# Two-half encoder trunk in split fp32: more pulled steps inside the normalisation chains, and a running LayerNorm sum in PSUM

## The chip, the cores and the metric

The kernel runs on one core of one Trainium2 chip. The metric is device time in microseconds. The kernel before took 1223.17 us (median of three runs, 1222.43 to 1230.81). Matmuls run on TensorE (PE), elementwise work on VectorE (DVE) and ScalarE (ACT), the splitting of weights on GpSimd (POOL), and nearly all transfers are issued by SyncE (SP).

## The reference

The input x is 512 positions by 1024 channels in fp32. Two layers are computed, and every sub-layer is x = x + RMSNorm(f(RMSNorm(x))).

```python
for i in range(DEPTH):                       # DEPTH = 2
    h = rms_norm(x, g[0])
    if i % 2 == 0:
        m = parallel_conv_mla(h, ...)        # short convolution beside latent attention
    else:
        m = conformer_conv(h, ...)           # pw1 -> GLU -> conv 31 -> LayerNorm -> silu -> pw2
    x = x + rms_norm(m, g[1])
    h = rms_norm(x, g[2])
    x = x + rms_norm(squared_relu_mlp(h, mlp_w1[i], mlp_w2[i]), g[3])

def conformer_conv(h, w_pw1, b_pw1, w_dw, b_dw, ln_g, ln_b, w_pw2, b_pw2):
    u = h @ w_pw1 + b_pw1
    a, g = jnp.split(u, 2, axis=-1)
    u = a * jax.nn.sigmoid(g)
    u = depthwise_conv(u, w_dw) + b_dw       # 31 taps per channel
    u = jax.nn.silu(layer_norm(u, ln_g, ln_b))   # LayerNorm over the 1024 channels
    return u @ w_pw2 + b_pw2
```

## The kernel before, in words

**Layout and arithmetic.** Channels lie on the 128 partitions in 8 tiles, positions along the free axis. Each fp32 operand is split into a high and a low part (`fp32r`), and each product is three matmuls (lines 244 to 246: high x high, low x high, high x low), so one output tile of 128 channels over 1024 input channels is a group of 24 matmuls. `strip` (line 208) fetches a weight strip of 128 x 1024, copies its high part on ACT (line 221) and subtracts it on POOL (line 222).

**The halves.** The positions are cut into half A (0 to 255) and half B (256 to 511). From the convolution on, A is 240 wide (`A2`) and B 272 wide (`B2`), since the 31 taps reach over the cut. All work of the second part of the program is a list of steps in the table `M2` (line 35): `up` and `down` are one output tile of an MLP product for one half (24 matmuls each), `pw1` is one tile of the gated product (48 matmuls), `pw2` one tile of the product after the LayerNorm. Between them stand the **chains** `join`, `norm` and `finish`: a sum of squares over all channels, a root, and a pass over eight tiles ("chunks") which gives the next product its input.

**A chain** is serial: the sum over partitions is a few matmuls with a column of ones (`done`, line 340; here called the SUM), the root is some twelve tiny instructions on DVE (`rstd`, lines 361 to 392), the result is spread over the partitions by matmuls with the identity (`spread`, line 406; the SPREAD), and then come the chunks: `join` has lines 444 to 462 before an MLP and 444 to 486 before another product, `layer_norm` lines 831 and 841 to 845. To keep PE busy meanwhile, the chain **pulls** steps of the other half out of the list and writes them into its own instruction stream. How many is set by `pace` (line 289): each chunk adds its estimated time to a clock, and one step is pulled whenever 2.9 us have come together (`STEP_US`, line 38).

**What sets the order.** In `M2` DVE works in the order in which the program writes its instructions. PE, ACT and POOL also work in order, in an order that the scheduler settles when the program is built. An `up` step is the group on PE, a relu on ACT (line 498), the square, a copy of the high part on ACT (line 228) and the subtraction on DVE (line 234), which is the last to read the step's PSUM bank. `up_step` (line 867) has the square done by ACT (line 500) while a convolution is under way, and otherwise by DVE (line 502). Groups inside a chain use only the three PSUM banks called S, since the banks pj, o and mi serve as the chain's scratch.

**Convolution.** The 31 taps per channel tile are 31 DVE instructions (lines 804 and 809) on a PSUM accumulator. They are dealt out between the steps by `fill` (line 274): each step gives a credit (`FILL`, line 40), and each tap costs `TAP_US` = 0.475 of it. When a `norm` chain begins, `layer_norm` adds up the eight convolved tiles on POOL (lines 820 and 821, executed at line 317) for the mean.

Of the kernel before, what the change touches and what calls it, by code (L numbers as in the profile page):

```python
# [34 lines left out]
M2 = [('up', 'A', 0, 0, 0, 8), ('join', 'B', 0, 1), ('down', 'A', 0, 0, 0, 8), ('up', 'A', 0, 1, 0, 8), ('down', 'A', 0, 1, 0, 8), ('up', 'A', 0, 2, 0, 8), ('down', 'A', 0, 2, 0, 8), ('up', 'A', 0, 3, 0, 8), ('down', 'A', 0, 3, 0, 8), ('join', 'A', 0, 3), ('up', 'B', 0, 0, 0, 8), ('down', 'B', 0, 0, 0, 2), ('pw1', 'A', 0, 4), ('down', 'B', 0, 0, 2, 6), ('pw1', 'A', 4, 8), ('down', 'B', 0, 0, 6, 8), ('up', 'B', 0, 1, 0, 8), ('down', 'B', 0, 1, 0, 8), ('up', 'B', 0, 2, 0, 8), ('norm', 'A'), ('down', 'B', 0, 2, 0, 8), ('pw2', 'A', 0, 8), ('join', 'A', 1, 1), ('up', 'B', 0, 3, 0, 8), ('down', 'B', 0, 3, 0, 8), ('join', 'B', 0, 3), ('up', 'A', 1, 0, 0, 8), ('down', 'A', 1, 0, 0, 8), ('pw1', 'B', 0, 3), ('up', 'A', 1, 1, 0, 8), ('pw1', 'B', 3, 6), ('down', 'A', 1, 1, 0, 8), ('pw1', 'B', 6, 8), ('up', 'A', 1, 2, 0, 8), ('down', 'A', 1, 2, 0, 8), ('norm', 'B'), ('up', 'A', 1, 3, 0, 8), ('pw2', 'B', 0, 8), ('join', 'B', 1, 1), ('down', 'A', 1, 3, 0, 8), ('up', 'B', 1, 0, 0, 8), ('down', 'B', 1, 0, 0, 6), ('finish', 'A'), ('down', 'B', 1, 0, 6, 8), ('up', 'B', 1, 1, 0, 8), ('down', 'B', 1, 1, 0, 8), ('up', 'B', 1, 2, 0, 8), ('down', 'B', 1, 2, 0, 8)]
# [94 lines left out]
def trunk(ctx: ExitStack, tc: tile.TileContext, a, out: bass.AP):  # L130
# [170 lines left out]
    class Sum:
# [128 lines left out]
    def join(xs, ms, s, post, pre, hs, seg, h, mlp):  # L430
# [695 lines left out]
```

## Time and profile before

| what | value |
|---|---|
| median of three runs | 1223.17 us |
| the profiled execution | 1222.25 us, of which its span is 1220.5 us |
| PE busy | 1160.9 us (95%) |
| DVE, ACT, POOL busy | 662.8, 654.1, 852.9 us (54%, 54%, 70%) |
| mean granted PE clock | 0.977 of full speed |

The page names each group by line, engine and operation; the table by stretches (the windows) gives for a piece of the span the busy time and, behind an x, the number of instructions of each engine, and then the granted PE clock. A matmul that waits is not counted as busy, and one at half clock counts as busy for twice as long, so in this kernel the number of matmuls in a stretch says more than the busy time.

### The profile page before, as it was taken

The numbers are of one execution on the slowest core, as the hardware profiler recorded it, in microseconds if no ns is written. First come the engines' busy times: TensorE is split into PE (matmuls) and PEld (weight loads), VectorE is DVE, ScalarE is ACT, GpSimd is POOL, SyncE is SP. The second block draws the span as 40 slices with busy tenths as digits, with TensorE's granted clock in tenths as the row PEclk, the third lists the DMA queues.
The fourth block names the chain that finished last, engine by engine and source line by source line (L and its number), as shares of the span: only waits on it lengthen the run. The fifth ranks groups of instructions, "written<-read, shape, count | busy, mean of one in ns | idle before, by whom it ended". The sixth has DMA issues, their size and how long they took to land.

```text
span 1220.5 us, 22995 instructions
## 1 busy us (share of the span) xinstructions
PE 1160.9 (95%) x8926; PEld 1118.3 (92%) x8926; DVE 662.8 (54%) x1707; ACT 654.1 (54%) x1181; POOL 852.9 (70%) x419
## 2 busy tenths in 40 slices
PE   7899989999999998999997989999999799999996
PEld 6788878999999998999997989999999799999995
DVE  5662699464512226678774455488896454232223
ACT  5421677466645446446456656564455666454351
POOL 5654563149888986789884848788988477778680
PEclk9899999999999999999998989999999899999998
DMA  6411332046555654455552635555556254564341
GB/s 213 148 59 38 98 100 69 2 158 211 189 189 174 205 183 149 155 191 187 187 177 90 197 99 190 171 192 192 192 185 191 72 188 156 184 179 155 117 160 37
DMA packets 55405, 184.01 MB, mean 151 GB/s; under 512 B 6400, under 2 KB 10880, under 8 KB 55296
## 3 DMA queue, kind: packets, MB, share of 16 engines
q1 hardware_dynamic: 54864, 182.00, 46.0%
q8 instruction: 70, 1.15, 0.4%
q10 hardware_dynamic: 432, 0.54, 0.1%
q14 instruction: 39, 0.32, 0.1%
HBM read 180.42 MB, written 2.10 MB: 150 GB/s over the span
## 4 chain that ended last, share of the span: by engine, by line
PE 84%; DVE 8%; ACT 4%; DMA 2%; issue 2%; POOL 1%; SPq 0%; DVEq 0%; ACTq 0%
PE S L244 21%; PE S L245 20%; PE S L246 20%; PE pj L244 6%; PE pj L245 6%; PE pj L246 6%; DMA raw<-in_win 1%; PE mi L340 1%; ACT whi L221 1%; POOL wlo L222 1%; DVE pr L744 1%; PE mi L406 1%; PE mi L747 1%; DVE s L738 1%; PE o L245 1%
## 5 line engine op out<-in xcount | busy, mean ns | idle before, releaser
L222 POOL TENSOR_TENSOR wlo<-raw,whi 128x1024 fp32r<-128x1024 f32 (+2 forms) x347 | 803.3, 2332 | 295.3 <-ACT whi L221 281.0
L221 ACT ACTIVATE whi<-raw 128x1024 fp32r<-128x1024 f32 (+2 forms) x347 | 355.9, 1030 | 405.6 <-PE S L245 198.1
L244 PE MATMUL S<-h,whi 128*128 128x256 f32 (+3 forms) x1224 | 357.6, 295 | 18.5 <-DVE hid L234 8.4
L246 PE MATMUL S<-h,wlo 128*128 128x256 f32 (+3 forms) x1224 | 357.6, 293 | 0.0
L245 PE MATMUL S<-h,whi 128*128 128x256 f32 (+3 forms) x1224 | 357.6, 293 | 0.0
L244 PEld LDWEIGHTS S<-h,whi 128*128 128x128 f32 x1224 | 235.1, 194 | 26.3 <-DVE hid L234 10.5
L246 PEld LDWEIGHTS S<-h,wlo 128*128 128x128 f32 x1224 | 236.2, 193 | 3.8 <-POOL wlo L222 0.2
L245 PEld LDWEIGHTS S<-h,whi 128*128 128x128 f32 x1224 | 236.1, 193 | 3.6 <-issue 0.2
L244 PE MATMUL S<-hid,whi 128*128 128x256 f32 (+2 forms) x808 | 227.5, 283 | 5.1 <-DVE acc L317 2.7
L245 PE MATMUL S<-hid,whi 128*128 128x256 f32 (+2 forms) x808 | 227.4, 282 | 0.0
L246 PE MATMUL S<-hid,wlo 128*128 128x256 f32 (+2 forms) x808 | 226.8, 281 | 0.0
L809 DVE SCALAR_TENSOR_TENSOR pj<-u,taps,pj 128x240 f32<-128x240 f32 (+1 forms) x464 | 192.7, 481 | 1.1
L244 PEld LDWEIGHTS S<-hid,whi 128*128 128x128 f32 x808 | 152.6, 190 | 6.7 <-DVE acc L317 3.5
L245 PEld LDWEIGHTS S<-hid,whi 128*128 128x128 f32 x808 | 153.3, 190 | 0.4 <-DVE hid L234 0.2
L246 PEld LDWEIGHTS S<-hid,wlo 128*128 128x128 f32 x808 | 153.1, 190 | 0.0
L244 PE MATMUL pj<-h,whi 128*128 128x272 f32 (+3 forms) x328 | 101.7, 310 | 6.5 <-ACT h L228 5.3
L245 PE MATMUL pj<-h,whi 128*128 128x272 f32 (+3 forms) x328 | 101.3, 309 | 0.0
L246 PE MATMUL pj<-h,wlo 128*128 128x272 f32 (+3 forms) x328 | 100.9, 308 | 0.0
L234 DVE TENSOR_TENSOR hid<-S,hid 128x256 fp32r<-128x256 f32 (+2 forms) x102 | 43.0, 421 | 62.2 <-ACT hid L228 62.2
L244 PEld LDWEIGHTS pj<-h,whi 128*128 128x128 f32 x328 | 62.5, 191 | 10.0 <-ACT h L228 5.6
L512 DVE TENSOR_TENSOR m<-S,m 128x256 f32<-128x256 f32 (+2 forms) x73 | 30.4, 417 | 70.1 <-PE S L246 70.1
L245 PEld LDWEIGHTS pj<-h,whi 128*128 128x128 f32 x328 | 62.4, 190 | 3.6 <-DVE h L231 0.9
(251 smaller groups left out, 1746.6 us busy)
## 6 DMA issues: line engine op xcount, KB each, us to landing
raw<-in_w SPq DMA_DIRECT2D x256, 512.0 KB, 3.4
raw<-in_pw SPq DMA_DIRECT2D x48, 512.0 KB, 3.5
raw<-in_win SPq DMA_DIRECT2D x16, 512.0 KB, 3.3
x<-in_xT SPq DMA_DIRECT2D x16, 256.0 KB, 4.1
raw<-in_wout SPq DMA_DIRECT2D x8, 512.0 KB, 3.3
raw<-in_wq SPq DMA_DIRECT2D x8, 192.0 KB, 2.4
out<-x SPq DMA_DIRECT2D x8, 120.0 KB, 4.1
out<-x SPq DMA_DIRECT2D x6, 136.0 KB, 1.8
```

The lines of the kernel that those rows point to most:

```text
L221: nc.scalar.activation(h, r, AF.Copy)
L222: nc.gpsimd.tensor_tensor(out=lo[:, c0:c1], in0=r, in1=h.bitcast(F32), op=ALU.subtract)
L234: eng.tensor_tensor(out=lo, in0=src, in1=hi.bitcast(F32), op=ALU.subtract)
L244: nc.tensor.matmul(acc, sh, mh, start=i == 0, stop=False)
L245: nc.tensor.matmul(acc, sh, ml, start=False, stop=False)
L246: nc.tensor.matmul(acc, sl, mh, start=False, stop=i == n - 1)
L340: nc.tensor.matmul(s[:, b : b + 1], q[:, sl.start - self.seg.lo : sl.stop - self.seg.lo], one, start=i == 0, stop=i == len(self.parts) - 1,)
L406: nc.tensor.matmul(o[:, sl], r[:, b : b + 1].to_broadcast([bw, P]), ident[:bw, :bw], start=True, stop=True,)
L512: nc.vector.tensor_tensor(out=m[seg.sl], in0=acc, in1=m[seg.sl], op=ALU.add)
L738: nc.vector.reduce_max(out=mx, in_=S, axis=AX.X)
L744: eng.tensor_scalar(out=pr_, in0=pr_, scalar1=sm, scalar2=None, op0=ALU.mult)
L809: nc.vector.scalar_tensor_tensor(out=dst, in0=src, scalar=wk, in1=acc, op0=ALU.mult, op1=ALU.add)
```

## The change

It does six things, all between the attention and the end.

1. **Holds.** A new `hold` runs at each sum and each root: it settles what is pending and pulls one step of the other half, whatever the clock says. `rstds` calls it ahead of the SUM and once more between root and SPREAD; `layer_norm` does the same around the mean, and `join` ahead of its last sum.
2. **Pace in operations.** The chain's clock counts DVE operations of 0.39 us and pulls at 2.35 us; the estimates for edges, roots and chunks are gone.
3. **Pulled squares.** `up_step` gives the square to ACT for pulled steps as well.
4. **LayerNorm's sum.** It runs along with the convolution: `Sum.run` copies the first convolved tile into the PSUM bank o on ACT and adds the others to it on DVE, each as the last action of its convolution; the last sum goes to SBUF. The POOL additions are gone, and the SUM of the mean has one part in place of two.
5. **Taps.** A tap costs 0.41 of credit in the 240-wide half and 0.44 in the 272-wide one.
6. **The table.** `M2` is reordered at the four places that the second block shows.

```diff
-STEP_US, EDGE_US, ROOT_US, CHUNK_US, SQUARE_US = 2.9, 1.0, 2.8, 1.45, 0.5
-TAP_US = 0.475
+OP_US, STEP_US = 0.39, 2.35
+TAP_US = {T // 2 - PAD: 0.41, T // 2 + PAD: 0.44}
...
+    def step():
+        if not steps or steps[0][0] or steps[0][1][1] in ("F", scope["half"]):
+            return False
+        scope["pulling"] = True
+        steps.pop(0)[2]()
+        scope["pulling"] = False
+        return True
+
+    def pace(n):
+        scope["time"] += n * OP_US
+        while scope["time"] >= STEP_US and step():
             scope["time"] -= STEP_US
         scope["time"] = min(scope["time"], STEP_US)
+
+    def hold():
+        settle()
+        if scope.get("chain") and step():
+            scope["time"] = 0.0
...
+        def run(self, t):
+            self.i += 1
+            if self.i == 1:
+                self.bank = ps("o")[:, : self.seg.w]
+                nc.scalar.activation(self.bank, t, AF.Copy)
+                self.parts = [self.bank]
+                return
+            dst = tmp("acc1")[:, : self.seg.w] if self.i == self.n else self.bank
+            self.eng.tensor_tensor(out=dst, in0=self.parts[0], in1=t, op=ALU.add)
+            self.parts = [dst]
...
     def rstds(total, ratio=None):
-        return spread(rstd(total.done(), D, ratio), total.seg)
+        hold()
+        r = rstd(total.done(), D, ratio)
+        hold()
+        return spread(r, total.seg)
...
-            pace(CHUNK_US)
+            pace(4 if mlp else 3)
...
-        vsum = Sum(NC, seg, nc.gpsimd, whole=WHOLE[1])
-        for c in range(NC):
-            vsum.add(vs[c][:, seg.sl])
+        hold()
         mu = small()[:, : seg.nb]
         nc.vector.tensor_scalar(
-            out=mu, in0=vsum.done(), scalar1=-1.0 / D, scalar2=None, op0=ALU.mult
-        )
+            out=mu, in0=vsum[seg].done(), scalar1=-1.0 / D, scalar2=None, op0=ALU.mult
+        )
+        hold()
...
-        scope["square"] = nc.scalar if convs or todo else nc.vector
+        scope["square"] = nc.scalar if convs or todo or scope.get("pulling") else nc.vector
```

```text
before: ('down','B',0,0,0,2), ('pw1','A',0,4), ('down','B',0,0,2,6), ('pw1','A',4,8), ('down','B',0,0,6,8)
after:  ('down','B',0,0,0,4), ('pw1','A',0,4), ('down','B',0,0,4,8), ('pw1','A',4,8)
before: ('norm','A'), ('down','B',0,2,0,8), ('pw2','A',0,8), ('join','A',1,1), ('up','B',0,3,0,8)
after:  ('norm','A'), ('down','B',0,2,0,8), ('up','B',0,3,0,4), ('pw2','A',0,8), ('join','A',1,1), ('up','B',0,3,4,8)
before: ('down','A',1,0,0,8), ('pw1','B',0,3), ('up','A',1,1,0,8), ('pw1','B',3,6), ('down','A',1,1,0,8)
after:  ('down','A',1,0,0,4), ('pw1','B',0,3), ('down','A',1,0,4,8), ('pw1','B',3,6), ('up','A',1,1,0,8)
before: ('down','A',1,2,0,8), ('norm','B'), ('up','A',1,3,0,8), ('pw2','B',0,8), ('join','B',1,1), ('down','A',1,3,0,8)
after:  ('norm','B'), ('down','A',1,2,0,8), ('up','A',1,3,0,4), ('pw2','B',0,8), ('join','B',1,1), ('up','A',1,3,4,8), ('down','A',1,3,0,8)
```

In each tuple the last two numbers are the range of tiles.

**What moves, place one: ACT, in the join of half A between the convolution module and the second MLP.** Names S_ are the accumulators of pulled `up` steps, y_ their relus, hid_ the copies of their high parts, whi_ weights, x_ and h_ the chain's own chunks. Before, the copy of a step stands behind the relu of a later step:

```order
L498 ACTIVATE y_8488<-S_8463 128x256
L450 ACTIVATE x_2173<-pj_8351 128x240
L459 ACTIVATE h_2189<-mi_8347 128x240
L450 ACTIVATE x_2174<-o_8393 128x240
L459 ACTIVATE h_2191<-pj_8351 128x240
L221 ACTIVATE whi_8699<-raw_8698 128x1024
L498 ACTIVATE y_8536<-S_8511 128x256
L228 ACTIVATE hid_8263<-S_8413 128x256
...
L498 ACTIVATE y_8576<-S_8551 128x256
L228 ACTIVATE hid_8265<-S_8463 128x256
```

Now relu, square and copy of one step follow each other (the lines are 22 to 27 higher in the changed file, L520 is the relu and L229 the copy):

```order
L520 ACTIVATE y_8482<-S_8457 128x256
L522 ACTIVATE S_8457<-y_8482 128x256
L229 ACTIVATE hid_7973<-S_8457 128x256
L222 ACTIVATE whi_8677<-raw_8676 128x1024
L520 ACTIVATE y_8527<-S_8502 128x256
L522 ACTIVATE S_8502<-y_8527 128x256
L229 ACTIVATE hid_7975<-S_8502 128x256
```

Over the whole program a relu stands ahead of an earlier step's copy 36 times before and 9 times now, among 128 `up` steps each.

**Place two: PE, at the second sum of the LayerNorm of half A.** Before, the SUM (L340, from the accumulated squares acc_ and sq_), the SPREAD (L406) and the first matmuls of `pw2` (inputs h_, 240 wide) follow each other:

```order
L246 MATMUL S_7896<-hid_7243,wlo_7694 128x256
L340 MATMUL mi_7867<-kst,acc_7742 128x1
L340 MATMUL mi_7867<-kst,sq_7865 128x1
...
L406 MATMUL mi_7887<-kst,s_7873 128x128 x2
L244 MATMUL S_7968<-h_2187,whi_7745 128x240
```

Now 18 matmuls of a pulled `down` step stand between SUM (L366) and SPREAD (L435), and four `up` steps of half B (96 matmuls, 256 wide) between SPREAD and `pw2`:

```order
L366 MATMUL mi_7804<-kst,sq_7770 128x1
L245 MATMUL S_7930<-hid_7257,whi_7737 128x256
...
L247 MATMUL S_7930<-hid_7267,wlo_7738 128x256
L435 MATMUL mi_7856<-kst,s_7810 128x128 x2
L245 MATMUL S_7985<-h_2187,whi_7773 128x256
...
L247 MATMUL S_8093<-h_2201,wlo_7926 128x256
L245 MATMUL pj_8129<-h_2187,whi_7980 128x240
```

**Place three: PE, at the same point of the LayerNorm of half B.** In the order before, SUM, SPREAD and `pw2` stand together as in half A. Now 39 matmuls of pulled steps lie between SUM and SPREAD, but `pw2` (272 wide) follows the SPREAD at once:

```order
L366 MATMUL mi_11621<-kst,sq_11567 128x1
L245 MATMUL S_11707<-h_2193,whi_11490 128x240
...
L247 MATMUL S_11758<-h_2201,wlo_11535 128x240
L435 MATMUL mi_11679<-kst,s_11629 128x128 x3
L245 MATMUL S_11835<-h_2187,whi_11644 128x272
```

The four `up` steps that cover half A's chunks are here pulled ahead of the SPREAD, because the rest of the taps has already taken five of the eight `down` steps.

More of the change, by code (lines that the diff above doesn't have):

```diff
@@ L32 @@
 N_RAW = 2
+PAD = 16
 M0 = [('wout', 'A'), ('join', 'A', 0, 1), ('wout', 'B')]
 M1 = []
[L35 removed]
@@ L36 @@
 M3 = [('up', 'B', 1, 3, 0, 8), ('down', 'B', 1, 3, 0, 8), ('finish', 'B')]
-STEP_US, EDGE_US, ROOT_US, CHUNK_US, SQUARE_US = 2.9, 1.0, 2.8, 1.45, 0.5
-TAP_US = 0.475
-FILL = {'up': 2.3, 'down': 2.3, 'first': 2.6, 'sum': 1.8, 'pw1': 4.8, 'pw2': 2.3, 'wout': 1.5}
+OP_US, STEP_US = 0.39, 2.35
+TAP_US = {T // 2 - PAD: 0.41, T // 2 + PAD: 0.44}
+FILL = {'up': 2.3, 'down': 2.3, 'first': 2.6, 'sum': 1.8, 'pw1': 4.8, 'pw2': 2.3}
 START = ['x', (128,), 'x', (256, 512, 768), 'x', 'x', 'x', 'x', 'x', 'x', ()]
@@ L277, in fill @@
         credit[0] += us
-        while convs and credit[0] >= TAP_US:
-            credit[0] -= TAP_US
+        while convs:
             turn[0] += 1
-            conv = convs[turn[0] % min(len(convs), 2)]
+            conv, cost = convs[turn[0] % min(len(convs), 2)]
+            if credit[0] < cost:
+                break
+            credit[0] -= cost
             if next(conv, None) is None:
-                convs.remove(conv)
+                convs.remove((conv, cost))
         if not convs:
@@ L811, in rest @@
                     )
-                yield k
-        convs.append(rest())
+                if k < CK - 1:
+                    yield k
+            vsum[seg].run(vs[c][:, seg.sl])
+            yield CK
+        convs.append((rest(), TAP_US[seg.w]))
     def layer_norm(seg):
         hv = views(hs, seg)
-        vsum = Sum(NC, seg, nc.gpsimd, whole=WHOLE[1])
-        for c in range(NC):
-            vsum.add(vs[c][:, seg.sl])
+        hold()
         mu = small()[:, : seg.nb]
         nc.vector.tensor_scalar(
-            out=mu, in0=vsum.done(), scalar1=-1.0 / D, scalar2=None, op0=ALU.mult
+            out=mu, in0=vsum[seg].done(), scalar1=-1.0 / D, scalar2=None, op0=ALU.mult
         )
+        hold()
         total = spread(mu, seg)
-        pace(EDGE_US)
         s2 = Sum(NC, seg, whole=WHOLE[2])
@@ L845, in layer_norm @@
             split((hv[c][0][seg.sl], hv[c][1][seg.sl]), t, nc.vector, late=late)
-            pace(2 * SQUARE_US)
+            pace(2)
         settle()
+    vsum = {}
     def start(c, seg):
+        if c == 0:
+            vsum[seg_of("AB"[seg is B], 1)] = Sum(NC, seg_of("AB"[seg is B], 1), nc.vector)
         if seg is A:
@@ L887, in shared_step @@
         down(kept[m], src(), ms[m], seg, first, sums[h])
-        fill(FILL["sum"])
     def pw1_step(tok, h, c):
```

33 lines of the change are left out of this document (7 added, 26 removed).

## Prediction

> **What bounds the kernel now.** I read the page first.
>
> ```profile
> PE 1160.9 (95%) x8926; PEld 1118.3 (92%) x8926; DVE 662.8 (54%) x1707; ACT 654.1 (54%) x1181; POOL 852.9 (70%) x419
> PE   7899989999999998999997989999999799999996
> PEclk9899999999999999999998989999999899999998
> ```
>
> PE sets the time; no other engine is above 70%. The slices show where it is not full: at the start and in the last slice, which the change doesn't touch, and in slices 16, 22, 24 and 32 (of 30.5 us each), with the clock down in three of these. How much is lost there the table by stretches tells, through the number of matmuls (behind the first x).
>
> ```profile
> 340.00:400.00 60.00, 60.00 (x511) 60.00 (x511) 13.04 (x31) 28.13 (x40) 49.55 (x21) 1.00 0.54 178
> 460.00:520.00 60.00, 54.64 (x439) 53.39 (x439) 41.53 (x114) 33.38 (x64) 41.62 (x18) 0.97 0.47 151
> 640.00:680.00 40.00, 31.76 (x249) 30.95 (x248) 15.64 (x52) 24.28 (x48) 22.23 (x11) 0.87 0.37 127
> 680.00:720.00 40.00, 33.99 (x243) 33.12 (x242) 22.46 (x66) 23.06 (x51) 23.41 (x10) 0.87 0.44 146
> 740.00:780.00 40.00, 38.65 (x332) 37.52 (x332) 26.16 (x80) 25.77 (x56) 29.15 (x13) 1.00 0.49 160
> 880.00:920.00 40.00, 40.00 (x359) 40.00 (x359) 37.15 (x93) 23.57 (x39) 35.63 (x18) 1.00 0.57 189
> 920.00:980.00 60.00, 51.09 (x394) 50.36 (x393) 30.92 (x86) 37.02 (x71) 36.38 (x17) 0.89 0.42 133
> 980.00:1020.00 40.00, 37.21 (x313) 36.28 (x312) 23.62 (x72) 26.37 (x55) 28.31 (x12) 1.00 0.52 166
> 1080.00:1140.00 60.00, 60.00 (x481) 60.00 (x480) 13.62 (x32) 27.61 (x42) 45.58 (x20) 1.00 0.44 142
> ```
>
> The first, sixth and last rows are undisturbed: 0.1174 us a matmul at 256 columns (60/511), 0.1114 at 240 (40/359), 0.1247 at 272 (60/481). What the other stretches lack at these rates is the loss. **a**, the join of A ahead of `pw1` (460 to 520): 511 - 439 = 72 matmuls, 8.5 us. **b**, the LayerNorm of A (640 to 680): some 62 wide and 187 narrow ones are worth 28.1 us, 11.9 lost. **c**, the join of A behind `pw2` (680 to 720): 28.4 us of work, 11.6 lost. **d**, the join of B ahead of `pw1` (740 to 780): about half of each width, 38.0, 2.0 lost. **e**, the LayerNorm of B (920 to 980): 24.4 + 21.8, 13.8 lost. **f**, the join of B behind `pw2` (980 to 1020): 35.8 at a mean of 0.1145, 4.2 lost. Together 52.0 us, all inside chains.
>
> **What PE waits for there**, from the table of waits (PE, 262 to 1200 us):
>
> ```profile
> PE S L244 <- DVE hid L234: 10.2, 10, 2.1
> PE mi L406 <- DVE s L392: 5.0, 2, 2.6
> PE mi L340 <- DVE acc L317: 4.8, 2, 3.1
> PE S L244 <- DVE u L786: 1.9, 1, 1.9
> ```
>
> **The change part by part.**
>
> *Holds in the LayerNorms (b, e).* PE's timeline, at the second sum of A's LayerNorm, then DVE's root and last chunk, and one window of the clock:
>
> ```profile
> 649.66 0.35 PE L340 MATMUL mi<-kst,acc 128*128 128x1 f32 x2 [3.14 <-DVE acc L317]
> 653.55 1.20 PE L406 MATMUL mi<-kst,s 128*128 128x128 f32 x4 [2.41 <-DVE s L392]
> 656.59 0.99 PE L244 MATMUL S<-h,whi 128*128 128x240 f32 x3 [1.85 <-ACT h L228]
> 651.18 0.16 DVE L361 TENSOR_SCALAR s<-mi 128x2 f32<-128x2 f32 x1 [1.35 <-PE mi L340]
> 653.25 0.16 DVE L392 SCALAR_TENSOR_TENSOR s<-mi,s 128x2 f32<-128x2 f32 x1
> 661.58 0.41 DVE L231 TENSOR_TENSOR h<-o,h 128x240 fp32r<-128x240 f32 x1 [0.44 <-ACT h L228]
> 652.50:655.00 2.50, 1.20 (x4) 0.93 (x4) 1.31 (x7) 0.00 (x0) 0.00 (x0) 0.50 0.03 13
> ```
>
> PE stands still for the sum, the root (651.18 to 653.41, 2.2 us) and the first chunk, and then takes the chunks at half clock as they come. Now the mean's SPREAD is followed by 81 matmuls, 9.5 us, against 7.1 us (642.6 to 649.7) of DVE work; the root has 18 matmuls beside it, 2.1 us; and the tail, 661.99 - 654.75 = 7.2 us, has four `up` steps, 96 x 0.1174 = 11.3 us. What stays open is the root. It is sometimes longer:
>
> ```profile
> 684.86 2.37 POOL L222 TENSOR_TENSOR wlo<-raw,whi 128x1024 fp32r<-128x1024 f32 x1 [0.53 <-ACT whi L221]
> 685.86 1.40 DVE L366 TENSOR_SCALAR s<-s 128x2 int32<-128x2 int32 x1
> 651.37 0.17 DVE L366 TENSOR_SCALAR s<-s 128x2 int32<-128x2 int32 x1
> ```
>
> One tiny instruction took 1.40 us and ended when POOL's subtraction did (687.23); at 651 POOL was idle and it took 0.17. Under a covered LayerNorm POOL keeps working, so I count a root of 2.2 to 4.4 us there, a wait of 0.1 to 2.3, and take 1.2. With 1.2 us for banks that the tail's steps share with the chain's scratch, b keeps 2.4 of 11.9: **-9.5**. (The Trainium skill, "SBUF — State Buffer", section "Who interferes with whom", says that DVE and GpSimd share a port pair, and whoever comes second waits for the whole instruction of the other. The trace agrees, with 687.26 against 687.23. It speaks against the change, which puts POOL work beside every root; by its worst case b would keep 3.5.)
>
> B's LayerNorm (e) has the same cover up to the SPREAD, and the root has 39 matmuls (4.3 us). Its tail has nothing:
>
> ```profile
> 954.89 1.28 ACT L844 ACT_TABLE_LOAD   x1
> 957.64 1.05 PE L244 MATMUL S<-h,whi 128*128 128x272 f32 x3 [2.89 <-ACT h L228]
> 487.66 1.01 PE L244 MATMUL S<-h,whi 128*128 128x256 f32 x3 [2.33 <-ACT h L228]
> 485.00:490.00 5.00, 2.67 (x14) 2.46 (x14) 2.50 (x7) 3.87 (x8) 3.81 (x2) 0.74 0.13 17
> 490.00:495.00 5.00, 5.00 (x41) 5.00 (x41) 3.35 (x9) 1.54 (x4) 0.88 (x1) 0.92 0.57 197
> ```
>
> The 2.9 us ahead of the first chunk stay, table load included. After the wait of 2.33 us in a the clock was 0.74 and then 0.92 over 5 us each: 2.6 + 0.8 = 3.4 us at half speed, 1.7 lost. I charge the same here, and 1.4 for the rest: e keeps 6.0 of 13.8, **-7.8**. (The Trainium skill, "TensorE: Matmul & The Clock Gate", section "Why this matters for your kernels", asks for no idle gap beyond about 3 us. By that the tail's 2.9 us might leave the clock alone, and the sum would be 1.7 lower; the row after 2.33 us disagrees.)
>
> *Pulled squares (c, and a, d).* ACT, DVE and PE in stretch c:
>
> ```profile
> 704.31 0.42 DVE L502 SCALAR_TENSOR_TENSOR S<-S,y 128x256 f32<-128x256 f32 x1
> 707.12 0.37 ACT L498 ACTIVATE y<-S 128x256 f32<-128x256 f32 x1
> 707.38 0.38 ACT L228 ACTIVATE hid<-S 128x256 fp32r<-128x256 f32 x1
> 707.79 0.42 DVE L234 TENSOR_TENSOR hid<-S,hid 128x256 fp32r<-128x256 f32 x1 [3.06 <-ACT hid L228]
> 708.26 0.39 PE L244 MATMUL S<-h,whi 128*128 128x256 f32 x1 [2.08 <-DVE hid L234]
> ```
>
> This is a circle. DVE has squared a step by 704.7; ACT may copy it only behind the relu of the step after the next, which waits for PE; DVE waits 3.06 us for the copy, with the chain's chunks queued behind, and PE 2.08 us for the bank that DVE frees. It comes again at 701 and 714. With the square on ACT the three operations stand together; only four of c's pulled steps are `up` now, the others `down`, which need one DVE addition. I leave c 3.0 (bank turns and the root), **-8.6**. In a, relu and copy stay crossed at one step; its tail has 10 matmuls behind the SPREAD and a whole `down` group further on, which shortens the wait of 2.33. The sigmoid wait of 1.9 stays, since its cause, two weight copies ahead of a table load, is in the new order too. a keeps 4.4 of 8.5, **-4.1**. d gains nothing that I can price, **0**; f has steps for its second half that were used up before, **-1.0**.
>
> *What this costs.* 30 squares go from DVE to ACT.
>
> ```profile
> 929.51 0.38 ACT L500 ACTIVATE S<-y 128x240 f32<-128x240 f32 x1
> 516.51 7.96 DVE L809 SCALAR_TENSOR_TENSOR pj<-u,taps,pj 128x240 f32<-128x240 f32 x21
> 807.78 4.17 DVE L809 SCALAR_TENSOR_TENSOR pj<-u,taps,pj 128x272 f32<-128x272 f32 x10
> L317 POOL TENSOR_TENSOR acc<-acc,m 128x272 f32<-128x272 f32 x5 | 3.9, 771 | 0.0
> ```
>
> At 0.38 us they are 11.4 us of ACT. ACT is busy 33.4 of 60 us in a and 25.8 of 40 in d, so most fit: 0 to 11.4, and I take **+2.5**.
>
> *Taps and the sum.* Taps come every 0.379 us (7.96/21) at 240 and 0.417 (4.17/10) at 272. A credit of 2.3 now buys 5.6 or 5.2 of them, 2.1 or 2.2 us of DVE, and with the 0.4 us subtraction 2.5 or 2.6 us per step, where PE needs 24 x 0.1174 = 2.8 or 24 x 0.1114 = 2.7. It fits, narrowly in B: 0. The POOL additions (12, 0.7 us each) leave an engine that isn't the bound; in their place come 14 DVE additions and two ACT copies, some 6 us that DVE has free beside the taps (37.2 of 40 us busy at the fullest): 0 to 6, I take 0. The SUM of the mean loses a part: under 1 us.
>
> **Sum.** -9.5 - 7.8 - 8.6 - 4.1 - 1.0 = -31.0; + 2.5 gives -28.5. On the profiled execution's 1222.25 us that is 1193.75; the median of the runs shown lies 0.92 above it, so I forecast 1194.7 us.
>
> **Rivals.**
>
> *The chains get longer (1209).* Each pulled step's last instruction stands on DVE ahead of the chain's next one and waits for PE. If sums and roots then come late, a SPREAD stalls PE, as L406 did twice for 2.5 us. For it: c's circle was of this kind. Against: behind a root every SPREAD but b's has at least 39 matmuls since its SUM. The six chains have twelve pairs of SUM and SPREAD; at half of that stall each, 1.2 us, they cost 14.4: 1209.
>
> *ACT takes over (1219).* If all 11.4 us of squares lie on the path, and the crossed pairs return as waits, a, c and d gain nothing: 1223.2 - 17.3 - 1.0 + 11.4 is 1216, and with b's root at its worst and the clock down once more some 1219. The rows speak against it: ACT is at 66% at most (f).
>
> *DVE falls behind the taps (1238, the other side).* A tap's duration in the table is above its spacing: 0.46 and 0.50. If the sum in PSUM or POOL's company spreads the taps to that, a step costs 5.6 x 0.46 + 0.4 + 0.1 = 3.1 and 5.2 x 0.50 + 0.5 = 3.1 us of DVE against 2.8 and 2.7: 0.3 and 0.4 us on each of some 45 steps, 31.5 us in all. Taps left over are drained when a LayerNorm begins and use up its steps: b then keeps e's 6.0 (+3.6) and e its 13.8 (+7.8). 1194.7 + 31.5 + 11.4 is 1238. It decides from 0.43 (A) and 0.42 us (B) per tap. Against: 21 taps in a row kept 0.379.
>
> *More is covered (1183).* If e's clock doesn't drop (1.7), no root meets POOL (1.2), banks never bind (1.2 in b, 1.4 in e), a and c keep only their fixed waits (4.0) and the squares are free (2.5), it is 12.0 lower.
>
> That the change doesn't pull what it says is excluded by the order of the instructions.
>
> **How the numbers follow.** Forecast 0.60, longer chains 0.15, more covered 0.10, DVE behind 0.08, ACT 0.07. The range runs from 1180, below the covered case, to 1214, past the longer chains; it leaves out the last two rivals and little else. A measurement of this kernel can tell about 1% (12 us) from no change. Faster by more: 0.60 + 0.10 + 0.12 of the longer chains = 0.82. Within 1%: 0.03 + 0.07 = 0.10. Slower: 0.08.
>
> **What would show it.** Right: stretches b and c without any window at clock 0.50, one left in e's tail with a wait near 2.9 us; L406 waits under 2 us in all; L234's waits as PE's releaser under 3 us; DVE near 95% busy while taps run, with PE at 20 of 20. Wrong: PE waits for DVE while taps run (the taps' rival), long L406 waits (the chains'), or weights and chunk copies late on ACT. The forecast fails altogether if the matmuls per 20 us in the undisturbed stretches change.

## The result, and the profile after

The changed kernel took **1191.6 us** (median of four runs, 1187.9 to 1199.8) against 1226.5 us for the kernel before (1222.4 to 1230.8): a ratio of 0.9724, 95% interval 0.9656 to 0.9792. The profiled execution took 1193.7 us, with a span of 1191.9 us. Set against the forecast of 1194.7 us that is 3.1 us less. By the ratio the gain is 25 to 42 us, in the medians 34.9, where 28.5 were forecast. So sign and size came out; but the terms of the sum were off in both directions, and two things that it put at nothing, the price of a tap and the taps that are left when a LayerNorm begins, were worth several us.

Three lines of the page: busy time of PE, its busy tenths in 40 slices of 29.8 us, and the granted clock.

```profile
PE 1149.6 (96%) x8916; PEld 1108.9 (93%) x8916; DVE 662.1 (56%) x1691; ACT 664.4 (56%) x1213; POOL 845.6 (71%) x407
PE   7899989999999999999998999999998999999996
PEclk9999999999999999999999999999989999999998
```

Of the four dips inside the convolution module's part, two are left: slice 22, the LayerNorm of A, now at full clock, and slices 30 and 31, the LayerNorm of B, where the clock is still lowered. The table by stretches shows it with numbers. The columns are the stretch, its length, the busy time and (x) the number of instructions on PE, weight loads, DVE, ACT and POOL, then the granted clock, the DMA share and GB/s.

```profile
460.00:520.00 60.00, 58.79 (x491) 58.02 (x491) 38.25 (x110) 37.98 (x75) 46.81 (x20) 1.00 0.53 172
520.00:560.00 40.00, 40.00 (x340) 40.00 (x340) 37.03 (x98) 20.59 (x32) 33.95 (x15) 1.00 0.56 188
640.00:665.00 25.00, 20.05 (x169) 19.47 (x168) 12.85 (x38) 17.77 (x34) 15.70 (x7) 1.00 0.43 140
665.00:720.00 55.00, 54.69 (x469) 54.28 (x468) 27.01 (x86) 37.62 (x78) 44.46 (x20) 1.00 0.56 182
720.00:780.00 60.00, 59.25 (x515) 58.60 (x514) 37.84 (x109) 40.49 (x82) 48.38 (x21) 1.00 0.54 173
880.00:920.00 40.00, 33.70 (x270) 33.17 (x268) 23.17 (x62) 21.53 (x37) 28.55 (x12) 0.90 0.47 152
920.00:945.00 25.00, 25.00 (x181) 24.90 (x181) 7.25 (x19) 17.04 (x33) 14.50 (x7) 0.89 0.37 122
945.00:1020.00 75.00, 73.53 (x619) 73.14 (x618) 35.29 (x98) 49.84 (x102) 57.24 (x25) 1.00 0.53 170
```

From such a row the loss is read as idle time plus busy time times what the clock lacked. In rows 6 and 7 (e, the LayerNorm of B) that is 6.3 + 33.7 x 0.10 + 25.0 x 0.11 = 12.4 us; in row 3 (b) it is 4.95 with the clock at 1.00, in row 4 (c) 0.3, in row 5 (d) 0.75, in row 1 (a) 1.2 and in the last (f) 1.5. Read over windows of 2.5 us, which is how the table further on was made, the kernel before lost 46.9 us by this measure (some 33 of idle time, some 14 of lowered clock) and the changed one 21.1 (15.2 and 5.9). That is 25.8 of the 28.6 us by which the span became shorter.

PE's waits, from 262 to 1150 us (sum, times, longest, all in us):

```profile
PE S L245 <- ACT h L229: 3.7, 1, 3.7
PE S L245 <- DVE m L534: 3.3, 3, 2.6
PE pj L245 <- DVE h L232: 2.3, 1, 2.3
PE mi L435 <- DVE s L421: 2.1, 1, 2.1
PE S L245 <- DVE u L808: 1.7, 3, 0.8
```

The first row of before's table, 10.2 us for `hid`, has no counterpart: the circle is gone. The second row, PE waiting for a `down` step's addition `m`, has grown: before it was 0.5 us. The timeline shows its cause, with b's two waits behind it (start, duration, engine and line, and in brackets the idle time before and its releaser):

```profile
877.19 7.60 DVE L831 SCALAR_TENSOR_TENSOR pj<-u,taps,pj 128x272 f32<-128x272 f32 x14
884.70 0.40 DVE L534 TENSOR_TENSOR m<-S,m 128x240 f32<-128x240 f32 x1
885.16 0.57 PE L245 MATMUL S<-hid,whi 128*128 128x240 f32 x1 [2.63 <-DVE m L534]
...
639.44 2.04 DVE L395 TENSOR_SCALAR s<-s 128x2 int32<-128x2 int32 x1
643.50 0.68 PE L435 MATMUL mi<-kst,s 128*128 128x128 f32 x4 [2.07 <-DVE s L421]
652.52 0.41 DVE L232 TENSOR_TENSOR h<-pj,h 128x240 fp32r<-128x240 f32 x1 [1.98 <-ACT h L229]
652.98 0.38 PE L245 MATMUL pj<-h,whi 128*128 128x256 f32 x1 [2.35 <-DVE h L232]
```

When B's LayerNorm begins, taps are left. The last `up` step has put five of them on DVE, and `norm_step` adds nine in two rounds before its clock, which starts at zero, reaches the 2.35 us at which it pulls a step. So 14 taps, 7.6 us, stand in one row ahead of the addition that frees a step's PSUM bank. PE stands for 2.63 us, and in this execution the clock follows:

```profile
882.50:885.00 2.50, 0.03 (x1) 0.00 (x0) 2.36 (x6) 1.06 (x1) 2.50 (x2) 0.90 0.31 62
885.00:890.00 5.00, 4.84 (x22) 4.84 (x23) 4.75 (x12) 0.00 (x0) 2.75 (x2) 0.50 0.73 238
890.00:892.50 2.50, 2.50 (x18) 2.50 (x18) 1.50 (x5) 1.06 (x1) 0.85 (x1) 0.74 0.22 90
```

That is 22 matmuls in 5 us, where 45 fit at the 240-wide rate. The same happens once more at the tail (some 919 to 925 us), behind the wait of 3.7 us. Of e's 12.2 us the row of taps is 5.7 (2.6 of idle time, 3.1 of clock) and the tail 6.3 (3.7 and 2.6).

### The profile page after: what moved, and what is told of

Its sections match the earlier page's. It is cut to its first block, busy times and chain, and to the rows that moved or that the text cites. A ratio compares the mean times of both kernels' runs of the same rounds, so it can differ in the third digit from the quotient of the medians.

```text
span 1191.9 us, 22942 instructions
## 1 busy us (share of the span) xinstructions
PE 1149.6 (96%) x8916; PEld 1108.9 (93%) x8916; DVE 662.1 (56%) x1691; ACT 664.4 (56%) x1213; POOL 845.6 (71%) x407
## 4 chain that ended last, share of the span: by engine, by line
PE 85%; DVE 6%; ACT 3%; DMA 2%; POOL 2%; issue 1%; SPq 0%; DVEq 0%; ACTq 0%; POOLq 0%
PE S L245 21%; PE S L246 21%; PE S L247 21%; PE pj L245 6%; PE pj L246 6%; PE pj L247 6%; POOL wlo L223 2%; DMA raw<-in_win 1%; ACT whi L222 1%; PE mi L366 1%; DVE pj L831 1%; DVE pr L766 1%; PE mi L435 1%; PE mi L769 1%; DVE s L760 1%
## 5 line engine op out<-in xcount | busy, mean ns | idle before, releaser
L245 PE MATMUL S<-h,whi 128*128 128x256 f32 (+3 forms) x1208 | 349.5, 291 | 7.0 <-ACT h L229 3.7
L247 PE MATMUL S<-h,wlo 128*128 128x256 f32 (+3 forms) x1208 | 350.2, 290 | 0.0
L246 PE MATMUL S<-h,whi 128*128 128x256 f32 (+3 forms) x1208 | 350.1, 290 | 0.0
L245 PE MATMUL S<-hid,whi 128*128 128x256 f32 (+2 forms) x840 | 237.2, 284 | 4.6 <-DVE m L534 2.8
L245 PEld LDWEIGHTS S<-h,whi 128*128 128x128 f32 x1208 | 228.8, 190 | 12.8 <-ACT h L229 3.9
L246 PE MATMUL S<-hid,whi 128*128 128x256 f32 (+2 forms) x840 | 236.4, 282 | 0.0
L247 PE MATMUL S<-hid,wlo 128*128 128x256 f32 (+2 forms) x840 | 236.2, 282 | 0.0
L247 PEld LDWEIGHTS S<-h,wlo 128*128 128x128 f32 x1208 | 229.6, 190 | 3.9 <-POOL wlo L223 0.4
L246 PEld LDWEIGHTS S<-h,whi 128*128 128x128 f32 x1208 | 229.4, 190 | 4.1 <-DVE h L232 0.3
L245 PEld LDWEIGHTS S<-hid,whi 128*128 128x128 f32 x840 | 159.2, 190 | 6.1 <-DVE m L534 3.2
L246 PEld LDWEIGHTS S<-hid,whi 128*128 128x128 f32 x840 | 159.8, 190 | 0.1
L247 PEld LDWEIGHTS S<-hid,wlo 128*128 128x128 f32 x840 | 159.6, 190 | 0.0
L245 PE MATMUL pj<-h,whi 128*128 128x272 f32 (+3 forms) x344 | 106.3, 309 | 8.7 <-ACT h L229 5.3
L246 PE MATMUL pj<-h,whi 128*128 128x272 f32 (+3 forms) x344 | 106.2, 309 | 0.0
L245 PEld LDWEIGHTS pj<-h,whi 128*128 128x128 f32 x344 | 65.6, 191 | 12.5 <-ACT h L229 5.7
L246 PEld LDWEIGHTS pj<-h,whi 128*128 128x128 f32 x344 | 65.5, 190 | 3.7 <-DVE h L232 0.9
```

Source lines behind the costliest of these rows:

```text
L245: nc.tensor.matmul(acc, sh, mh, start=i == 0, stop=False)
L246: nc.tensor.matmul(acc, sh, ml, start=False, stop=False)
L247: nc.tensor.matmul(acc, sl, mh, start=False, stop=i == n - 1)
```

## The experiments

Losses in us by stretch, each the sum over 2.5 us windows of idle time + busy time x (1 - clock), in the profiled execution; the bounds of e and f follow each kernel's own place of the LayerNorm. All rows share the bound between b and c, at 665 us; in runs 5 and 6 the clock that b's waits lowered comes back later, and 1.8 and 1.0 us of b's stand under c.

| kernel | a | b | c | d | e | f | sum | median (lowest to highest), us | ratio to before, interval |
|---|---|---|---|---|---|---|---|---|---|
| before | 6.9 | 11.5 | 10.7 | 1.4 | 13.6 | 2.8 | 46.9 | 1223.5 to 1227.2 in the comparisons | 1 |
| after | 1.2 | 5.1 | 0.3 | 0.8 | 12.2 | 1.5 | 21.1 | 1191.6 (1187.9 to 1199.8) | 0.9724, 0.9656 to 0.9792 |
| 1, squares back | 3.1 | 8.5 | 1.7 | 5.0 | 9.8 | 4.6 | 32.7 | 1205.6 (1205.6 to 1206.2) | 0.9849, 0.9805 to 0.9894 |
| 2, squares alone | 5.0 | 11.0 | 0.6 | 0.0 | 9.6 | 2.8 | 29.0 | 1202.6 (1202.1 to 1214.2) | 0.9846, 0.9784 to 0.9908 |
| 3, no holds | 5.3 | 7.1 | 5.1 | 4.5 | 14.7 | 6.3 | 43.0 | 1218.1 (1212.8 to 1226.0) | 0.9952, 0.9918 to 0.9987 |
| 4, old table | 3.6 | 5.1 | 0.0 | 0.3 | 6.8 | 1.0 | 16.8 | 1192.2 (1188.2 to 1198.1) | 0.9754, 0.9690 to 0.9819 |
| 5, sum on POOL | 1.2 | 8.0 | 2.1 | 0.8 | 9.0 | 1.5 | 22.6 (+8.1 at 300) | 1201.4 (1191.3 to 1203.9) | 0.9775, 0.9718 to 0.9832 |
| 6, old tap price | 1.0 | 10.5 | 1.3 | 0.8 | 13.9 | 1.5 | 29.0 | 1200.7 (1199.5 to 1202.4) | 0.9786, 0.9746 to 0.9825 |
| 7, LayerNorm B later | 1.2 | 5.1 | 0.3 | 0.8 | 5.2 | 1.5 | 14.1 | 1189.4 (1188.3 to 1190.4) | 0.9694, 0.9648 to 0.9740 |
| 8, LayerNorm B at its old place | 1.2 | 5.1 | 0.3 | 0.8 | 5.4 | 1.0 | 13.8 | 1188.8 (1187.8 to 1198.8) | 0.9706, 0.9651 to 0.9760 |
| 9, root from PSUM | 1.2 | 4.1 | 0.3 | 1.9 | 10.9 | 1.5 | 19.9 | 1193.6 (1189.8 to 1196.1) | 0.9740, 0.9702 to 0.9777 |
| 10, 7 and 9 together | 1.2 | 5.7 | 0.3 | 1.9 | 6.9 | 1.3 | 17.3 | 1189.8 (1188.6 to 1192.2) | 0.9714, 0.9681 to 0.9747 |
| 11, before with 9's root | 5.7 | 12.2 | 8.3 | 0.9 | 13.6 | 2.8 | 43.5 | 1219.5 (1215.7 to 1221.2) | 0.9951, 0.9928 to 0.9973 |
| 12, 5 and 9 together | 1.2 | 5.7 | 0.3 | 1.9 | 10.0 | 1.5 | 20.6 | 1193.9 (1191.1 to 1196.1) | 0.9729, 0.9693 to 0.9765 |

### 1 and 2: the squares of pulled steps

```diff
-        scope["square"] = nc.scalar if convs or todo or scope.get("pulling") else nc.vector
+        scope["square"] = nc.scalar if convs or todo else nc.vector
```

The first run takes this condition out of the changed kernel; the second puts it alone into the kernel before.

> The changed kernel with one condition as before: the squares of pulled steps stand on DVE again, wherever no taps are left. Theory (the circle DVE square - ACT copy behind a later relu - DVE waits - PE waits costs most of stretch c and part of a): PE waits for hid return with some 6 to 10 us in sum, the stretch from 680 to 720 us loses at least 5 us again, and the time is 8 to 12 us above the changed kernel's 1191.6: 1200 to 1204 us. Rival (the steps pulled behind pw2 are now half down steps, so the circle cannot close anyway, and the squares' place is worth nothing): within 2 us of 1191.6, and no wait for hid above 1 us in sum.

> The kernel before with one edit alone: squares of pulled steps on ACT. Theory: stretch c loses 8 us less, a one or two less, the LayerNorms (b, e) stay as they were: 1213 to 1217 us against 1226.5, PE waits for hid near 0, half-clock windows at 650 and 930 us stay. Rival (squares are worth nothing without the reordered steps): 1224 to 1228 us.

Measured: taken back, 1205.6 us, 14 us above the changed kernel. Alone, 1202.6 us (1202.1 to 1214.2), a ratio that is worth 11 to 26 us. Both medians moved by more than the theories said (8 to 12 and some 10 to 13 us), and both rivals, by which the squares' place is worth nothing, are out. Where the second run gains is the place that the forecast named, from 665 us on the join of A behind `pw2`, and d beside it:

```profile
665.00:720.00 55.00, 54.35 (x467) 54.06 (x466) 28.06 (x84) 40.88 (x91) 45.24 (x20) 1.00 0.53 173
720.00:780.00 60.00, 60.00 (x530) 59.93 (x529) 25.62 (x79) 39.23 (x83) 51.54 (x23) 1.00 0.58 193
```

c fell from 10.7 to 0.6 there, e by another 4.0 (half of it idle time, half clock; the cause was not traced), and b, whose chain had no steps beside it, stayed at 11.0. In the first run, however, c lost only 1.7, and PE's waits for `hid` were 2.5 us in sum. So the circle itself does not come back among `down` steps; the squares cost something else. The groups by line on DVE, from 440 to 1040 us, first of the run with the squares back, then of the changed kernel (count, busy us and mean ns, then the idle time ahead of them and its releaser):

```profile
L524 DVE SCALAR_TENSOR_TENSOR S<-S,y 128x240 f32<-128x240 f32 (+2 forms) x35 | 14.7, 419 | 19.5 <-ACT y L520 19.5
```

```profile
L524 DVE SCALAR_TENSOR_TENSOR S<-S,y 128x272 f32<-128x272 f32 (+1 forms) x7 | 3.1, 440 | 7.5 <-ACT y L520 7.5
```

DVE stands 19.5 us ahead of 35 squares, waiting for the relu on ACT, with the chain's instructions queued behind, against 7.5 us ahead of seven. The losses turn up where a join and pulled `up` steps meet (a +1.9, c +1.4, d +4.2, f +3.1), 3.3 of these 10.6 us by the clock. b's +3.4 is not of this kind: A's LayerNorm pulls `down` steps alone, its idle time grew by 0.3 us, and the rest is a lowered clock behind the same 2.07 us of wait for the root and a second wait of 3.1 us. Whether the squares bring that about is not shown.

### 3: no steps by sums and roots

```diff
     def hold():
         settle()
-        if scope.get("chain") and step():
-            scope["time"] = 0.0
```

> The changed kernel without the steps that are put unconditionally by each sum and root (a hold only settles the taps' credit, and the pace by DVE instructions is all that pulls). Theory (the sum of 7 us and the root of 2 us on DVE must have steps beside them): b and e lose some 4 to 5 us more each and the joins 1 to 2: 1200 to 1206 us, PE waits for the root (spread of s) of 2 us each return. Rival (the pace pulls the same steps a little later, nothing lost): 1190 to 1194 us.

Measured: 1218.1 us, far above the range of the theory: no more than 0.1 to 0.8% below the kernel before. The expectation forgot that the same diff also takes out the old estimates for edges and roots (`EDGE_US`, `ROOT_US`): without the holds nothing pulls a step at a sum or root, where the kernel before still did. PE's waits, 262 to 1150 us:

```profile
PE S L245 <- DVE hid L235: 10.8, 6, 2.3
PE mi L433 <- DVE s L419: 6.7, 2, 4.3
PE S L245 <- DVE m L532: 5.7, 5, 2.6
```

The wait for a root's result is 4.3 us, and steps wait behind chains on DVE instead. So the pulls at sums and roots carry some 26 us, but part of this only stands in place of what the old pace did, and no run separates the two. What the holds add to the old pace is nearer to the distance of the second run from the changed kernel, 11 us in the medians, the other edits counted in.

### 4, 7 and 8: the table, and where B's LayerNorm begins

The fourth run has the whole table `M2` of before. In the other two only the end of the new one is changed:

```text
after: ('norm','B'), ('down','A',1,2,0,8), ('up','A',1,3,0,4), ('pw2','B',0,8), ('join','B',1,1), ('up','A',1,3,4,8), ...
7:     ('down','A',1,2,0,4), ('norm','B'), ('down','A',1,2,4,8), ('up','A',1,3,0,6), ('pw2','B',0,8), ('join','B',1,1), ('up','A',1,3,6,8), ...
8:     ('down','A',1,2,0,8), ('norm','B'), ('up','A',1,3,0,8), ('pw2','B',0,8), ('join','B',1,1), ('down','A',1,3,0,8), ...
```

> The changed kernel with the order of steps of before (the last down group of B's half, and of A's, not spread around the LayerNorm and pw2). Theory: the LayerNorm of A has its cover but no up steps for its tail; the LayerNorm of B has up steps where the changed order has down steps; c has only up steps. b and c lose some 3 to 8 us more together, e some 2 to 4 us less: 1193 to 1199 us. Rival (which step is pulled does not matter, only that one is): 1190 to 1193 us. A second rival (the reordered steps carry most of the gain): 1205 us and above.

> The changed kernel with B's LayerNorm placed four steps later (behind half of the down group), and six up steps instead of four kept for its tail. By the instruction order no burst of taps is left then: the taps stand five or six beside each step. Theory (the 14 taps in a row on DVE ahead of a step's addition cost e 2.6 us of wait and a half-clock stretch): e loses 6 to 8 us instead of 12.4, no PE wait for the addition m above 1 us, 1184 to 1190 us. Rival (e's loss is its tail, which this does not change): 1190 to 1194 us.

> The changed kernel with B's LayerNorm at its old place alone (behind the whole down group, eight up steps behind it, the next down group behind the join), the other places of the table as in the change. Theory: as with the half-way place, no burst; up steps cover the tail as they do in the run with the whole old table, where e lost 6.4 us: 1184 to 1190 us. Rival (up steps need ACT three times a step, and ACT's copies then stand ahead of the tail's chunks): e loses 8 us or more, 1190 to 1196 us.

Measured: the whole old table gives 1192.2 us, the first rival's range, so the reordering carries none of the gain that can be measured. But its stretches are not those of the changed kernel: e lost 6.8 us instead of 12.2, and a 3.6 instead of 1.2. The reordering gave at a and took back at e. With the LayerNorm of B four or eight steps later, e falls to 5.2 and 5.4 and all else stays, within half a us. In the seventh run the same taps on DVE stand beside the steps:

```profile
877.44 2.66 DVE L831 SCALAR_TENSOR_TENSOR pj<-u,taps,pj 128x272 f32<-128x272 f32 x5
880.01 0.40 DVE L534 TENSOR_TENSOR m<-S,m 128x240 f32<-128x240 f32 x1
880.33 2.73 DVE L831 SCALAR_TENSOR_TENSOR pj<-u,taps,pj 128x272 f32<-128x272 f32 x5
882.97 0.40 DVE L534 TENSOR_TENSOR m<-S,m 128x240 f32<-128x240 f32 x1
```

and its stretch e has no window below full clock:

```profile
880.00:920.00 40.00, 35.09 (x304) 34.22 (x303) 24.64 (x68) 24.98 (x44) 30.30 (x13) 1.00 0.51 168
920.00:945.00 25.00, 24.66 (x196) 24.24 (x197) 6.68 (x17) 17.11 (x32) 17.50 (x9) 1.00 0.48 148
```

The longest wait for `m` is 0.8 us there. The tail is better covered too. In place of PE's wait of 3.7 us there are two, of 1.1 and 1.0 us, and not because of the steps alone: the table load of the activation function stands earlier on ACT. First the changed kernel, then the seventh run:

```profile
916.53 1.28 ACT L864 ACT_TABLE_LOAD   x1
```

```profile
913.39 1.28 ACT L864 ACT_TABLE_LOAD   x1
```

In the changed kernel a weight copy and a pulled step's relu hold ACT until the load begins, 0.6 us behind the end of the SPREAD (915.89), and the first chunk's copy ends at 919.51, 3.6 us behind it. In the seventh run the load is over before the SPREAD ends (913.99), the copy ends at 916.09, 2.1 us behind it, and 24 matmuls of a pulled `up` step fill that time. So e's loss was the row of taps and the tail together. It fell by 7.0 us in the profiled executions, 1.1 of it idle time and 5.9 clock, of which their spans show 4.9 (1191.9 to 1187.0). In time it is 1189.4 and 1188.8 us against 1191.6, with intervals that overlap: the best medians of the study, and no difference that these runs can prove.

### 6: the price of a tap

```diff
-TAP_US = {T // 2 - PAD: 0.41, T // 2 + PAD: 0.44}
+TAP_US = {T // 2 - PAD: 0.475, T // 2 + PAD: 0.475}
```

> The changed kernel with a tap counted at 0.475 us in both halves instead of 0.41 and 0.44. Fewer taps are put beside each step, so that more are left when a LayerNorm begins: by the instruction order all eight steps of the down group are then used up beside leftover taps in both LayerNorms, against none in A and five in B now. Theory (leftover taps take the steps that should cover the chain): b loses 3 to 6 us more, e 1 to 4 us more, 1196 to 1202 us. Rival (fewer taps per step relieve DVE, and that pays for it): 1188 to 1193 us.

Measured: 1200.7 us, the theory's range; 9 us above the changed kernel. PE at the LayerNorm of A:

```profile
656.11 0.35 PE L366 MATMUL mi<-kst,acc 128*128 128x1 f32 x2 [4.38 <-DVE acc L331]
659.75 1.19 PE L435 MATMUL mi<-kst,s 128*128 128x128 f32 x4 [2.40 <-DVE s L421]
662.78 0.99 PE L245 MATMUL S<-h,whi 128*128 128x240 f32 x3 [1.85 <-ACT h L229]
```

These are the three waits of the kernel before (3.14, 2.41 and 1.85), come back, holds or no holds: the leftover taps have used up the eight steps that should have stood beside the chain. With what stands under c, b loses 11.5 us again.

### 5, 9, 10, 11 and 12: the LayerNorm's sum, and the root

In the fifth run the LayerNorm's sum is six POOL additions at its begin again.

> The changed kernel with the LayerNorm's sum as before: six additions on POOL at the LayerNorm's begin instead of DVE additions into PSUM as each channel group's taps end. Theory (the prediction's: POOL's 12 additions of 0.7 us each are 4.2 us per LayerNorm behind which steps stand, so the place of the sum is worth nothing by itself): 1190 to 1196 us. Rival (each LayerNorm begins 4 us later in the chain while the steps run out at its tail): 4 us per LayerNorm on the path, 1198 to 1202 us.

Measured: 1201.4 us, which looks like the rival. The profile says otherwise. First the run with the sum on POOL, then the changed kernel, at a join long before any LayerNorm:

```profile
287.97 16.44 POOL L223 TENSOR_TENSOR wlo<-raw,whi 128x1024 fp32r<-128x1024 f32 x7
295.21 9.22 DVE L395 TENSOR_SCALAR s<-s 128x2 int32<-128x2 int32 x1
306.44 1.19 PE L435 MATMUL mi<-kst,s 128*128 128x128 f32 x4 [6.27 <-DVE s L421]
```

```profile
289.59 19.02 POOL L223 TENSOR_TENSOR wlo<-raw,whi 128x1024 fp32r<-128x1024 f32 x8
295.87 0.83 DVE L395 TENSOR_SCALAR s<-s 128x2 int32<-128x2 int32 x1
```

An instruction on 128x2 numbers took 9.22 us and ended at 304.43, when POOL's row of seven subtractions did (304.41). PE waited 6.27 us, and half clock followed: 8.1 us lost, before the edit under test has any effect. To take this out of the comparison, the root was changed: the guess that was worked out from SBUF into SBUF is copied from the one in PSUM.

```diff
-        guess(r)
         guess(q)
+        nc.vector.tensor_copy(r, q)
```

> The changed kernel with one instruction of the root replaced: the first guess of each reciprocal root is no longer worked out from SBUF into SBUF (the int32 instruction that took between 0.17 and 9.22 us at one place in the runs so far), but copied from the guess in PSUM, an instruction that took 0.16 us in every root. Theory (that one instruction waits for POOL's weight subtractions, back to back, and this makes the root 2.2 to 4.4 us and more, from run to run): no root above 2.4 us, PE's wait for the root ahead of A's second LayerNorm spread (2.07 us now) gone or under 0.3 us, 1185 to 1190 us, and the runs within 5 us of each other instead of 12. Rival (the wait moves to the next instruction of the root, or PE waits for something else then): 1190 to 1194 us and the same spread.

> The changed kernel with the LayerNorm's sum on POOL again and the root's first guess copied from PSUM, against the same root with the sum in PSUM (1193.6, 1189.8 to 1196.1). The run with the sum on POOL alone had 9.22 us in one int32 instruction at 295 us, long before any LayerNorm. Theory (the sum's place is worth nothing; that run's 1201.4 was the root's stall): 1190 to 1196 us. Rival (the sum on POOL costs 4 us per LayerNorm, whatever the root does): 1199 to 1203 us.

> The changed kernel with B's LayerNorm four steps later and the root's first guess copied from PSUM. Theory: both add up; of the 14.1 us in which PE stood still with the later LayerNorm alone, the two waits for a root (3.6 us) go: 1184 to 1188 us. Rival (the waits for the first chunk behind a root only become longer by as much): 1188 to 1190 us.

> The kernel before with the root's first guess copied from PSUM. Theory: its int32 instructions lose 9 us in sum on DVE, of which the LayerNorms' own were short already (0.17 and 0.31 us); joins gain 3 to 6 us: 1220 to 1224 us against 1226.5, with less spread than 12 us. Rival: no change, 1225 to 1229 us.

The groups by line from 250 to 1240 us, of the changed kernel and of the ninth run:

```profile
L395 DVE TENSOR_SCALAR s<-s 128x2 int32<-128x2 int32 (+1 forms) x16 | 13.7, 854 | 0.6
```

```profile
L403 DVE COPY s<-mi 128x2 f32<-128x2 f32 (+1 forms) x15 | 2.4, 160 | 0.5
```

The stalls are gone (160 ns in the mean), and with them PE's wait of 2.07 us in b (0.3 is left). The time of the changed kernel stayed: 1193.6 us, the rival's range. The runs lie closer, 6 us instead of 12. In the kernel before the same edit is worth 3 to 9 us (ratio 0.9928 to 0.9973), about the theory's 3 to 6, and the runs lie within 5.5 us instead of 13. With the later LayerNorm it adds nothing (1189.8, the rival's range). With the sum on POOL the time is 1193.9 us against 1193.6: **the place of the LayerNorm's sum is worth nothing**, and the 1201.4 us of the fifth run are not its doing. Its profiled execution shows the root's stall; the other runs that were near 1201 us have no profile, so for them the cause is inferred from the twelfth run.

## Why the prediction was right, and where it was wrong

**The whole.** Forecast 28.5 us less, measured 28.5 on the profiled executions (1222.25 to 1193.72), 34.9 in the medians. That the first pair agrees so closely is luck: terms that were too large and too small met, and 5.9 us of the changed profile are clock, which differs from run to run.

**a, join A ahead of `pw1`: too small.** It was to keep 4.4 of 8.5 us; 491 of 511 matmuls stand in its 60 us, which leaves 2.3 by the forecast's own count and 1.2 by idle time. The wait of 2.33 us, which was only to become shorter, is gone, and the one behind the sigmoid, which was to stay at 1.9, is 0.8 at the longest. The whole old table leaves 3.6 of idle measure here, so of the 5.7 us that a gained the reordered `pw1` steps are some 2.4 and the other edits 3.3.

**b, LayerNorm A: too large.** It was to keep 2.4; it kept 5.1, all of it idle, at full clock. The root with POOL busy was within its bounds: 2.04 us for the one instruction, 2.07 us of wait where 1.2 was charged. Too small was the tail. Not four `up` steps but two, 48 matmuls, stand between the SPREAD (643.50) and the wait of 2.35 us at 652.98. The third has the bank pj, which is the chain's scratch, and has to wait until a chunk has been read from it. For such banks 1.2 was charged.

**c, join A behind `pw2`: too small,** 0.3 kept instead of 3.0. The circle was read rightly: the squares alone took c from 10.7 to 0.6 us in the kernel before.

**d and f: a little too small.** d was held to gain nothing and went from 1.4 to 0.8; f was to gain 1.0 and went from 2.8 to 1.5. In the run with the squares alone d fell to nothing, so squares delayed it too.

**e, LayerNorm B: the step that failed.** The forecast let it keep 6.0, with "the same cover up to the SPREAD" as in A. It kept 12.2 of 13.6. The tail was sized about rightly: 6.3 us, where the wait, its clock and the rest were charged with 6.0. What the sum put at nothing is the row of taps, 5.7 us. Moving B's LayerNorm eight `down` steps forward left it the last taps, which those steps had carried on DVE. That leftover taps take `down` steps was known, and was held against the tail's cover alone; what they do on the queue that frees a step's bank was not asked. By DVE's order four of the eight steps are used up while taps drain (additions at 884.70, 887.05, 889.94 and 891.13); the fifth, at 893.76, is the one that the hold at the mean pulls in any case. How much the row costs is in part chance: in the first run the same row (7.61 us) and the same wait (2.63 us) left the clock at 1.00 (rows in the last section), which makes 2.6 us of it.

The rival in which DVE falls behind the taps named this mechanism ("Taps left over are drained when a LayerNorm begins and use up its steps") and priced it at 7.8 in e, not far from these 5.7; only its condition was not needed. It takes no taps that are slower beside every step, only fewer steps ahead of the LayerNorm. That the row's own taps took 0.54 us each did make it worse: at the forecast's 0.417 it would be 1.8 us shorter, and PE's wait, by estimate, 0.9 us. With the LayerNorm moved back by four steps, e kept 5.2.

**Taps by their real length: not nothing.** The sum had them at 0. At the old price the time is 9 us longer and b loses what it lost before (11.5). The 9.5 us that the forecast gave to the holds in b rest on the tap price as much: with leftover taps there is no step to hold with.

**Squares: cost and worth.** The +2.5 us on ACT cannot be told apart from nothing. The worth was undersized: the forecast had 12.7 us in a and c; alone the edit is worth 11 to 26 us and taking it back costs 14, 10.6 of it lost at a, c, d and f, since squares that wait for ACT hold up DVE in every join, not in c's circle only. Everything but the squares is worth 13 to 24 us (the first run). The two add up to a little more than the whole, 34 us by the ratio.

**The LayerNorm's sum: nothing, as forecast,** once the root's stall is out of the way.

**What was to show it.** Stretches b and c have no window at half clock, the wait for `hid` is gone, and in 520 to 560 us DVE is busy 37.03 of 40 us with PE at 40.00: as forecast. The root's waits on PE are 2.1 us, just past the bound of 2. e has two half-clock stretches, not one, and a tail wait of 3.7 instead of 2.9 us.

**What stays open.** What the holds are worth by themselves: the third run takes away the old pulls at sums and roots with them. Why the ninth run did not get faster, although the 2 us wait in b went, is not settled: d lost 1.1 us more, e's clock loss differed, and both are within what runs of one kernel differ by.

## What to carry to other kernels

When a chain is moved ahead of steps, count what those steps carried on every engine, not only the matmuls that they lend as cover: work left over lands at the chain's begin, in one row on the queue that frees the banks. A parameter that only paces filler work (here the price of a tap) can be worth as much as the edit that it serves, so it belongs into the sum with the term that rests on it. Where runs of one kernel differ by a per cent, look for the instruction whose duration differs at one place from run to run, and take it out before comparing small edits.

## What the runs showed of the hardware

**A tiny DVE instruction can lose several turns to POOL.** The guess from SBUF into SBUF at one place, near 295 us, took 0.37, 0.83, 1.14, 4.03, 1.61, 0.76, 9.22, 1.67, 0.69 and 3.04 us in ten profiled executions (before, after and runs 1 to 8), always beside a row of POOL subtractions; the copy from PSUM took 0.16. The Trainium skill, "SBUF — State Buffer", section "Who interferes with whom", says that a DVE instruction in a two-port mode and a GpSimd instruction exclude each other for the whole instruction. That the guess runs in such a mode no run shows. The trace agrees in that the guess is held up beside POOL's row, and goes further: 9.22 us is nearly four of POOL's subtractions (16.44/7 = 2.35 us each) and ends with the last of them, so here DVE did not get in between them.

**The same gap has either clock behind it.** PE's wait for the root in b was 2.07 us in the changed kernel and in the first run. In the former the clock stayed at 1.00 and the four matmuls of the SPREAD took 0.68 us (row above); in the latter they took 0.94, and half clock followed:

```profile
644.48 0.94 PE L435 MATMUL mi<-kst,s 128*128 128x128 f32 x4 [2.07 <-DVE s L421]
```

```profile
645.00:647.50 2.50, 2.50 (x13) 2.50 (x13) 1.28 (x4) 1.60 (x4) 0.85 (x1) 0.50 0.30 66
647.50:650.00 2.50, 2.50 (x21) 2.50 (x20) 1.52 (x5) 1.21 (x4) 0.00 (x0) 0.87 0.41 162
```

So the same wait cost nothing more in one execution and some 1.6 us in the other (2.5 x 0.50 + 2.5 x 0.13). It is the same with PE's wait behind the row of 14 taps, 2.63 us in both: in the changed kernel the clock fell to 0.50, in the first run it stayed.

```profile
895.50 0.38 PE L245 MATMUL S<-hid,whi 128*128 128x240 f32 x1 [2.63 <-DVE m L534]
895.00:897.50 2.50, 2.00 (x17) 2.01 (x18) 2.39 (x7) 0.00 (x0) 2.50 (x2) 1.00 0.69 231
```

The changed kernel's four runs had mean clocks of 0.991, 0.990, 0.986 and 0.984 in the order of their times, 1187.9, 1189.5, 1193.7 and 1199.8 us. By estimate, 0.7% of the clock is 8 of the 12 us between them.

**Taps of one tile in a row are slower.** The 14 taps of that row, which by the instruction order all add to one accumulator, took 0.54 us each (7.60/14); rows of five in the seventh run, at the same place, took 0.53 (2.66/5). Where taps of two tiles alternate, the forecast's row of ten has 0.417. Nothing was run on this alone, and POOL was busy in both.
